# One PSUM bank of a projection taken from another pool: a two-layer hybrid decoder trunk on one NeuronCore

## The chip, the cores and the metric

The kernel runs on one core of a Trainium2 chip. The metric is the device time of one execution in microseconds; the other cores are idle. The engines are named as in the profile: PE (TensorE, matrix multiply; PEld is its weight load), DVE (VectorE), ACT (ScalarE), POOL (GpSimd) and SP (SyncE, which here only issues DMAs). PE accumulates into PSUM, which has eight banks of 128 partitions by 512 float32 in this kernel's use; DVE and ACT read the results out.

## What is computed

512 tokens of width 1024 go through two layers. In each layer one normalised input `h` feeds a gated short convolution (A), a sparse attention with an indexer and a top-k choice of 128 keys (B), a gated linear recurrence in chunks (C) and a cross-attention into 256 memory tokens (M). Each branch is lifted to width 1024, gated, and summed; then come an output projection, a residual, and a SwiGLU feed-forward part with a residual. Cut to what the change touches:

```
h = rmsnorm(x, norm_mix)
(..., d_q, d_k, d_v, ..., g_q, g_f, g_i, g_g, m_q, gate_logits) = split_cols(h @ w_in)
hv  = g_i.reshape(b, s, HG_HEADS, HG_DV)          # the recurrence's values
o_c = hgrn2_chunkwise(hq, hk, hv, log_f)
y_b = dsa_attention(q, k, d_v, iq, ik, iw)        # 8 heads of 64, 4 blocks of 128 queries
merged = sum over n of gates[:, :, n] * (branches[n] @ w_lift[n])
```

## The kernel before, in words

**Products.** All large products are float32 made of three passes of a rounded type: each operand is split into a high and a low part, and `mm3` (L271 to L276) issues high by high, high by low, low by high. A weight matrix comes in chunks (`Chunk`, L214 to L230): SP issues one DMA into `w_raw` (two buffers of 1 MB), then for each piece of 128 by 1024 numbers ACT makes `w_hi` (L226) and DVE makes `w_lo` (L229), three buffers each. Both have a raised priority (AHEAD). In `features` the weight is the stationary operand, so L274 and L275 read `w_hi` and L276 reads `w_lo`. In `tokens_wide` the tokens are stationary and the weight streams.

**Names in the trace.** In a trace row the left name is the tile written and the right ones are read. A row such as `mm<-h_hi,w_hi` does not say which of the two was stationary.

**PSUM.** The eight banks are three pools, each tile one bank: `mm` with three (L103, accumulators of the products), `at` with two (L106, the scores of the attentions) and `tr` with three (L109, transposes and small sums).

```
MM_BUFS = 3
TR_BUFS = 3
AT_BUFS = 2
```

**Values.** `values` (L682 to L691) makes the four token blocks of `hv` from one 1024 by 512 slice of `w_in`. It needs four accumulators at once, one for each block of 128 tokens: the three `mm` banks and one more. `tokens_wide` (L261) walks the four weight pieces and adds each into all four accumulators. ACT then scales every accumulator into `hv` (L688). The first three of these are put into `behind`, and the next `w_hi` pass is ordered after them (L227); the fourth is not.

**Attention.** `attend(t)` (L705 to L738) handles a block of 128 queries in two halves of four heads. For each head, `dots` (L700) issues two small products into an `at` bank (L702, L703), DVE adds the bias, finds the smallest and writes `prob` (L715; five buffers), ACT takes the exponential, DVE inverts the sum (L718), ACT scales. Then PE transposes the four `prob` tiles into `tr` banks (L726), which frees them, and multiplies with the values of the attention into another `tr` bank (L732).

```
for i in range(4):
    ps = at_ps()[:, :n]
    dots(ps, qS, kS, 4 * q + i, t, n)
    p = dp2.tile([P, S], F32, name="prob", bufs=PR_BUFS)[:, :n]
    dve.tensor_tensor_reduce(out=p, in0=ps, in1=biases[t], ...)
```

**What sets the order.** L868 writes the program order of the stage: `values`, then three halves of `attend`, then one step of the lift of branch A (gates, L529, and products, L546), three more halves, and so on. A scheduler takes instructions at compile time by priority (this program order, and AHEAD for the marked ones), engine by engine, as soon as its own model of the timeline holds them ready; it hands out the buffers of a pool in the same walk. The result is one fixed list for each engine, and on the chip each engine works its list strictly in order and waits where a buffer or an input is not there yet. Just ahead of the stage DVE works the last top-k search of the indexer (`select`, L841, L842).

The stage runs once in each layer, at about 307 to 455 us and 1291 to 1440 us of the span.

Of the kernel before, what the change touches and what calls it, by code (L numbers as in the profile page):

```python
# [45 lines left out]
MM_BUFS = 3  # L46
# [23 lines left out]
def hybrid_trunk(ctx: ExitStack, tc: tile.TileContext, x, mem, positions, norm_mix, w_in, conv_w,  # L70
# [19 lines left out]
    def A(dst, src, func, **kw):  # L90
        name = tables.get(func)
        if name is not None and name != table["set"]:
            load = act.preload_act_table_set(name)
            for u in table["users"]:
                tc.add_manual_dep(load.ins, u.name, order, reason="table set")
            table.update(set=name, load=load.ins, users=[])
        i = act.activation(dst, src, func, **kw)  # L97
        if name is not None:
            tc.add_manual_dep(i.ins, table["load"].name, order, reason="table set")
            table["users"].append(i.ins)  # L100
        return i

    def mm_ps():  # L103
        return pmm.tile([P, 512], F32, name="mm")

    def at_ps():  # L106
        return pat.tile([P, 512], F32, name="at", bufs=AT_BUFS)

    def tr_ps():  # L109
        return pat.tile([P, 512], F32, name="tr", bufs=TR_BUFS)  # L110
# [129 lines left out]
    def wchunk(src, kt, n):  # L240
        return Chunk(src, kt, n)
# [19 lines left out]
    def tokens_wide(ws, a, kt, pss):  # L261

        k0 = 0
        for w in ws:
            for ks, _, _ in w.parts:
                for t, ps in enumerate(pss):
                    for k in ks:
                        mm3(ps, pair(a, k0 + k, slice(t * P, (t + 1) * P)), w.at(k), k0 + k == 0, k0 + k == kt - 1)
            k0 += w.kt
# [246 lines left out]
    def mixer(l, h, norms, cm, cf):  # L516
# [164 lines left out]

        def values(hv):  # L682
            ws = [wchunk(w_in[l][k0 * P:(k0 + 4) * P, C_GI:C_GI + 512], 4, 512) for k0 in (0, 4)]
            pss = [mm_ps() for _ in range(MM_BUFS)] + [at_ps()]
            tokens_wide(ws, h, KD, pss)
            for t, ps in enumerate(pss):
                with tc.high_priority(offset=AHEAD):
                    i = A(hv[:, t, :], ps, AF.Copy, scale=r_t[:, t:t + 1])  # L688
                if t < MM_BUFS:
                    behind.append(i)  # L690
            yield  # L691

        with pool_("dsa") as dp:
# [173 lines left out]
            with pool_("att", "left") as dp2:  # L867
                weave(chain(values(hv), lift(0, y_a, merged)), chain(*(attend(t, dp2, y_b) for t in range(NT))), R2)  # L868
# [268 lines left out]
```

## Time and profile before

| what | value |
|---|---|
| median of 3 runs | 2047.54 us (2046.99 to 2047.55) |
| the profiled execution | 2047.71 us |
| span of its instructions | 2045.6 us |
| PE busy | 2031.7 us, 99% of the span |
| DVE busy | 1277.0 us, 62% |
| ACT busy | 1019.9 us, 50% |
| mean DMA rate | 100 GB/s |
| granted TensorE clock, mean | 0.997 |

A row of the timeline gives start, duration, engine, line, operation, tiles, and in brackets the idle time of the engine just before with the instruction that ended it. Matmuls overlap in the pipeline, so their durations overlap too; the distance from one start to the next is what a matmul costs PE. A row of the windows gives the stretch, its length, then busy time (and instructions) of PE, PEld, DVE, ACT and POOL, the granted clock, the share of DMA, and GB/s.

### The profile page before, as it was taken

What the parts mean: (1) busy time and instruction counts of PE and PEld (TensorE: products, weight loads), DVE (VectorE), ACT (ScalarE), POOL (GpSimd) and SP (SyncE); (2) the same over time, 40 slices, a digit from 0 to 9 for tenths busy, and PEclk for the clock granted to TensorE, in tenths of its full rate; (3) what the DMA queues carried; (4) which work ended last, traced back from release to release, by engine and by line L of the source; (5) the groups of instructions that cost most, each with busy time, mean ns of one, the idle gap of its engine ahead of it and who ended that gap; (6) DMA issues with size and microseconds to landing.
All of it is one profiled execution on the core that took longest, in us unless ns stands there. A gap on an engine that the chain in (4) does not pass through costs nothing.

```text
span 2045.6 us, 26194 instructions
## 1 busy us (share of the span) xinstructions
PE 2031.7 (99%) x10156; PEld 1705.9 (83%) x10156; DVE 1277.0 (62%) x2519; ACT 1019.9 (50%) x1836; POOL 9.8 (0%) x33
## 2 busy tenths in 40 slices
PE   8999999999999999999999999999999999999999
PEld 8998987778888888888889898877888788888887
DVE  6779997657686544344457889864777654533442
ACT  7653655866665433223355456486766633322231
POOL 0000000000000000000000000000000000000000
PEclk9999999999999999999999999999999999999999
DMA  7623232212243232233243213222222422323222
GB/s 251 221 85 97 68 103 83 81 54 93 68 128 113 83 103 93 93 104 102 88 155 94 88 57 108 88 62 83 83 83 83 145 87 98 103 73 113 92 83 93
DMA packets 185660, 203.77 MB, mean 100 GB/s; under 512 B 4271, under 2 KB 172289, under 8 KB 185409
## 3 DMA queue, kind: packets, MB, share of 16 engines
q1 hardware_dynamic: 181248, 193.04, 29.7%
q10 hardware_dynamic: 4128, 8.93, 1.2%
q8 instruction: 80, 1.31, 0.3%
q14 instruction: 44, 0.35, 0.1%
q0 software_dynamic: 160, 0.13, 0.0%
HBM read 191.60 MB, written 10.49 MB: 99 GB/s over the span
## 4 chain that ended last, share of the span: by engine, by line
PE 97%; DMA 1%; DVE 1%; ACT 1%; issue 0%; SPq 0%; DVEq 0%
PE mm L274 29%; PE mm L275 29%; PE mm L276 29%; PE tr L732 1%; PE tr L726 1%; PE at L702 1%; PE at L703 1%; PE at L276 1%; PE at L274 1%; PE at L275 1%; DMA w_raw<-in_mem_w_kv_dram 1%; PE at L954 0%; PE at L980 0%; PE tr L668 0%; PE tr L771 0%
## 5 line engine op out<-in xcount | busy, mean ns | idle before, releaser
L229 DVE TENSOR_TENSOR w_lo<-w_raw,w_hi 128x1024 fp32r<-128x1024 f32 (+1 forms) x346 | 419.5, 1213 | 383.2 <-ACT w_hi L97 383.0
L274 PE MATMUL mm<-h_hi,w_hi 128*128 128x512 f32 x1664 | 651.9, 393 | 0.7 <-DVE fg L1081 0.4
L275 PE MATMUL mm<-h_lo,w_hi 128*128 128x512 f32 x1664 | 651.6, 392 | 0.0
L276 PE MATMUL mm<-h_hi,w_lo 128*128 128x512 f32 x1664 | 649.8, 392 | 0.0
L97 ACT ACTIVATE w_hi<-w_raw 128x1024 fp32r<-128x1024 f32 (+1 forms) x346 | 363.2, 1051 | 463.2 <-PE mm L275 397.5
L274 PEld LDWEIGHTS mm<-h_hi,w_hi 128*128 128x128 f32 x1664 | 313.2, 188 | 65.0 <-DVE fg L1081 1.2
L276 PEld LDWEIGHTS mm<-h_hi,w_lo 128*128 128x128 f32 x1664 | 312.9, 188 | 64.6 <-issue 0.6
L275 PEld LDWEIGHTS mm<-h_lo,w_hi 128*128 128x128 f32 x1664 | 313.1, 188 | 63.3 <-issue 1.0
L276 PE MATMUL mm<-w_hi,h_lo 128*128 128x256 f32 (+2 forms) x368 | 109.5, 298 | 0.0
L275 PE MATMUL mm<-w_lo,h_hi 128*128 128x256 f32 (+2 forms) x368 | 109.1, 297 | 0.0
L274 PE MATMUL mm<-w_hi,h_hi 128*128 128x256 f32 (+2 forms) x368 | 108.3, 298 | 0.0
L275 PE MATMUL mm<-a_lo,w_hi 128*128 128x512 f32 x272 | 106.1, 390 | 0.0
L274 PE MATMUL mm<-a_hi,w_hi 128*128 128x512 f32 x272 | 105.9, 389 | 0.0
L276 PE MATMUL mm<-a_hi,w_lo 128*128 128x512 f32 x272 | 105.6, 390 | 0.0
L274 PE MATMUL mm<-y_hi,w_hi 128*128 128x512 f32 x256 | 100.4, 393 | 1.2 <-ACT y_hi L97 1.2
L275 PE MATMUL mm<-y_lo,w_hi 128*128 128x512 f32 x256 | 100.7, 393 | 0.0
L276 PE MATMUL mm<-y_hi,w_lo 128*128 128x512 f32 x256 | 100.3, 392 | 0.0
L97 ACT ACTIVATE a_hi<-fg 128x512 fp32r<-128x512 f32 x44 | 27.8, 633 | 106.9 <-DVE fg L1086 106.9
L97 ACT ACTIVATE prob<-prob,small 128x256 f32<-128x256 f32 (+3 forms) x128 | 69.0, 554 | 14.7 <-DVE small L715 8.6
L275 PEld LDWEIGHTS mm<-w_lo,h_hi 128*128 128x128 f32 x368 | 70.2, 191 | 2.2
L276 PEld LDWEIGHTS mm<-w_hi,h_lo 128*128 128x128 f32 x368 | 70.2, 191 | 1.9
L274 PEld LDWEIGHTS mm<-w_hi,h_hi 128*128 128x128 f32 x368 | 69.9, 191 | 1.9
(377 smaller groups left out, 2982.9 us busy)
## 6 DMA issues: line engine op xcount, KB each, us to landing
w_raw<-in_w_in_dram SPq DMA_DIRECT2D x72, 1024.0 KB, 5.2
w_raw<-in_ffn_w_up_dram SPq DMA_DIRECT2D x44, 1024.0 KB, 5.1
w_raw<-in_w_lift_dram SPq DMA_DIRECT2D x32, 512.0 KB, 3.5
w_raw<-in_ffn_w_down_dram SPq DMA_DIRECT2D x16, 1024.0 KB, 5.3
w_raw<-in_mem_w_kv_dram SPq DMA_DIRECT2D x8, 1024.0 KB, 5.4
w_raw<-in_w_out_dram SPq DMA_DIRECT2D x8, 1024.0 KB, 5.4
w_raw<-in_ffn_w_down_dram SPq DMA_DIRECT2D x10, 512.0 KB, 3.4
kv<-kv ACTq DMA_DIRECT2D x8, 512.0 KB, 3.2
```

What stands on the lines that cost most here:

```text
L97: i = act.activation(dst, src, func, **kw)
L229: dve.tensor_sub(lo, raw[:, k:e], f(hi))
L274: pe.matmul(ps, ah, bh, start=first, stop=False)
L275: pe.matmul(ps, ah, bl, start=False, stop=False)
L276: pe.matmul(ps, al, bh, start=False, stop=last)
L702: pe.matmul(ps, q[:, hh, s], k[0][:, :n], start=True, stop=False)
L703: pe.matmul(ps, q[:, hh, s], k[1][:, :n], start=False, stop=True)
L726: pe.transpose(pp[:, (2 * e + i) * P:(2 * e + i + 1) * P], probs[2 * i + e][:, b * P:(b + 1) * P], ident)
L732: pe.matmul(pv[e * HD:(e + 1) * HD, :], vt[:, b, :], pt[:, b, e * 2 * P:(e + 1) * 2 * P], start=b == 0, stop=b == t)
```

## The change

One line of `values`: its fourth accumulator is a tile of the pool `tr` in place of one of the pool `at`. Nothing else is edited; sizes and numbers of buffers stay, and no instruction is added or taken away. `final` (L1047), which also uses an `at` bank as a fourth accumulator, stays as it is.

```
         def values(hv):
             ws = [wchunk(w_in[l][k0 * P:(k0 + 4) * P, C_GI:C_GI + 512], 4, 512) for k0 in (0, 4)]
-            pss = [mm_ps() for _ in range(MM_BUFS)] + [at_ps()]
+            pss = [mm_ps() for _ in range(MM_BUFS)] + [tr_ps()]
             tokens_wide(ws, h, KD, pss)
```

More of the change, by code (lines that the diff above doesn't have):

```diff
@@ L683, in values @@
             ws = [wchunk(w_in[l][k0 * P:(k0 + 4) * P, C_GI:C_GI + 512], 4, 512) for k0 in (0, 4)]
-            pss = [mm_ps() for _ in range(MM_BUFS)] + [at_ps()]
+            pss = [mm_ps() for _ in range(MM_BUFS)] + [tr_ps()]
             tokens_wide(ws, h, KD, pss)
```

## The prediction, made before the change was run

> **What bounds the kernel now.** I read the page first, then the waits of PE, then the windows and the timeline around the two places where `values` runs.
>
> ```profile
> span 2045.6 us, 26194 instructions
> PE 2031.7 (99%) x10156; PEld 1705.9 (83%) x10156; DVE 1277.0 (62%) x2519; ACT 1019.9 (50%) x1836; POOL 9.8 (0%) x33
> PE 97%; DMA 1%; DVE 1%; ACT 1%; issue 0%; SPq 0%; DVEq 0%
> ...
> PE at L702 <- DVE small L715: 2.4, 6, 0.4
> PE mm L274 <- ACT y_hi L97: 1.2, 1, 1.2
> ```
>
> PE is busy all but 14 us, and the chain that ends last is PE for 97%. So the time is PE's list of matmuls plus its waits, and a wait taken out of PE's list comes off the end unless another takes its place. The longest entry of PE's waits is six waits of the attention's scores (L702) for the DVE reduction L715. The busy shares of the two stages that hold them are in the windows:
>
> ```profile
> 1305.00:1330.00 25.00, 23.83 (x112) 19.52 (x111) 17.05 (x45) 11.97 (x27) 0.00 (x0) 1.00 0.28 85
> 1330.00:1440.00 110.00, 110.00 (x561) 85.87 (x560) 61.84 (x142) 81.73 (x163) 1.49 (x4) 1.00 0.23 72
> ```
>
> Of the 25 us around the end of `values` PE lacks 1.17 us; in the 110 us after it, none. DVE has 61.84 of 110 us to do there and ACT 81.73. The timeline of PE in layer 1 shows where the 1.17 us are:
>
> ```profile
> 1311.57 0.22 PE L702 MATMUL at<-k_hi,qS 128*128 128x128 f32 x1
> ...
> 1317.02 0.39 PE L276 MATMUL at<-w_hi,h_lo 128*128 128x512 f32 x1
> 1317.24 0.22 PE L702 MATMUL at<-k_hi,qS 128*128 128x128 f32 x1
> 1317.30 0.28 PE L703 MATMUL at<-k_lo,qS 128*128 128x128 f32 x1
> 1317.97 0.33 PE L702 MATMUL at<-k_hi,qS 128*128 128x128 f32 x1 [0.39 <-DVE small L715]
> ...
> 1318.80 0.33 PE L702 MATMUL at<-k_hi,qS 128*128 128x128 f32 x1 [0.39 <-DVE small L715]
> ...
> 1319.63 0.33 PE L702 MATMUL at<-k_hi,qS 128*128 128x128 f32 x1 [0.39 <-DVE small L715]
> 1319.79 0.28 PE L703 MATMUL at<-k_lo,qS 128*128 128x128 f32 x1
> 1319.90 0.45 PE L274 MATMUL mm<-h_hi,w_hi 128*128 128x512 f32 x1
> ...
> 1320.87 0.39 PE L276 MATMUL mm<-h_hi,w_lo 128*128 128x512 f32 x1
> ...
> 1322.03 0.39 PE L275 MATMUL mm<-h_lo,w_hi 128*128 128x512 f32 x1
> ...
> 1324.98 0.22 PE L702 MATMUL at<-k_hi,qS 128*128 128x128 f32 x1
> ...
> 1325.38 0.45 PE L275 MATMUL mm<-h_lo,w_hi 128*128 128x512 f32 x1
> ```
>
> The first head's dots run at 1311.57, inside `values`. The last product of `values` starts at 1317.02. Then heads two to five go through one bank, each waiting for the reduction of the one before, and the first gate product (L274) comes at 1319.90. One `at` bank is enough to keep them apart by 0.83 us because the other still holds the fourth accumulator, as ACT's rows show:
>
> ```profile
> 1316.31 0.69 ACT L97 ACTIVATE hv<-mm,rstd_t 128x512 f32<-128x512 f32 x1 [0.44 <-PE mm L276]
> 1316.90 1.99 ACT L97 ACTIVATE w_hi<-w_raw 128x1024 fp32r<-128x1024 f32 x2
> ...
> 1319.17 0.68 ACT L97 ACTIVATE hv<-at,rstd_t 128x512 f32<-128x512 f32 x1
> ```
>
> The fourth accumulator is read out from 1319.17 to 1319.85, so for the whole stall the scores have a single bank.
>
> **The change, part by part.** No instruction is added or removed; a bank moves. Two things follow.
>
> First, the scores have two banks throughout. From 1317.24 to 1319.90 are 2.66 us for four heads. What four heads cost without waits: two of them run from 1324.98 to 1325.38, 0.40 us, so four take 0.80. The stall is thus worth 1.86 us in layer 1, more than the 1.17 us that the records call idle, since their ends are modelled. In layer 0 the same four heads take 333.02 to 335.69, 2.67 us (rows below). Upper bound of the gain: 2 x 1.86 = 3.7 us.
>
> It will not all come back, because the next work, the first gate product, needs weights. DVE's rows:
>
> ```profile
> 1316.33 0.28 DVE L715 CUSTOM_DVE_ANT_0 prob<-at,causal_bias 128x128 f32<-128x128 f32 x1
> ...
> 1317.62 0.29 DVE L715 CUSTOM_DVE_ANT_0 prob<-at,causal_bias 128x128 f32<-128x128 f32 x1 [0.99 <-PE at L703]
> ...
> 1319.49 1.22 DVE L229 TENSOR_TENSOR w_lo<-w_raw,w_hi 128x1024 fp32r<-128x1024 f32 x1
> ...
> 1326.89 0.29 DVE L715 CUSTOM_DVE_ANT_0 prob<-at,causal_bias 128x128 f32<-128x128 f32 x1 [3.38 <-PE tr L726]
> ...
> 1328.61 1.22 DVE L229 TENSOR_TENSOR w_lo<-w_raw,w_hi 128x1024 fp32r<-128x1024 f32 x1 [1.42 <-ACT w_hi L97]
> ```
>
> ACT's first `w_hi` starts at 1316.90 and is one of two in 1.99 us, so it is there at about 1317.9. The pass for `w_lo` takes 1.22 us, and the first product that reads `w_lo` (L276, 1320.87) follows its end (1319.49 + 1.22 = 1320.71) by 0.16. If DVE turns to `w_lo` the moment `w_hi` is there, L276 can start at 1317.9 + 1.22 + 0.16 = 1319.3, 1.6 us earlier than now. I expect two reductions ahead of it instead (head one and two are then reduced from 1316.33 on, under the tail of `values`; three and four follow at 1317.62, about 0.3 us each), so `w_lo` runs from 1318.25 to 1319.47 and L276 starts at 1319.63: 1.24 us earlier. By that point six heads are done instead of five, which saves 0.20 later: 1.44 to 1.8 us a layer. I take 1.6, so **3.2 us** for both layers. Lower bound: if one bank-sized wait is all that goes, a 0.83 us step becomes 0.20, 0.6 us a layer, 1.2 in all; a loss is bounded under the rivals.
>
> Does the earlier start carry to the end? What stands in its way would be weights for the following products. The next `w_lo` pass of this stage that matters starts at 1328.61 and ends at 1329.83; its chunk is first used here:
>
> ```profile
> 1339.45 0.40 PE L274 MATMUL mm<-h_hi,w_hi 128*128 128x512 f32 x1
> ```
>
> That is 9.6 us of cover, against 1.6 us of shift. I cost the knock-on at nothing; without that cover each shifted microsecond would be lost again, at most 3.2.
>
> Second, a `tr` bank is held until about 1319.85 (335.6 in layer 0). Who waits for it? The first row is the readout of the fourth accumulator in layer 0, the second the busy time of all instructions on `tr` tiles from 318 to 335.6 us, the third the first transpose of the stage in layer 1:
>
> ```profile
> 334.95 0.67 ACT L97 ACTIVATE hv<-at,rstd_t 128x512 f32<-128x512 f32 x1
> ...
> 318.00:335.60 17.60, 0.00 (x0) 0.00 (x0) 0.00 (x0) 0.00 (x0) 1.00 0.10 31
> ...
> 1326.58 0.27 PE L726 MATMUL tr<-ident,prob 128*128 128x128 f32 x1
> ```
>
> No one uses `tr` in that time, and the first user comes 6.7 us after the bank is free, with two other banks beside it. Cost: nothing. Were the transposes to come straight after `values`, two banks in place of three would hold a transpose back for one readout, 0.68 us.
>
> Third, the clock, in layer 0 only:
>
> ```profile
> 333.02 0.22 PE L702 MATMUL at<-k_hi,qS 128*128 128x128 f32 x1
> ...
> 335.69 0.49 PE L274 MATMUL mm<-h_hi,w_hi 128*128 128x512 f32 x1
> 335.97 0.63 PE L275 MATMUL mm<-h_lo,w_hi 128*128 128x512 f32 x1
> ...
> 339.38 0.39 PE L275 MATMUL mm<-h_lo,w_hi 128*128 128x512 f32 x1
> ...
> 335.00:337.00 2.00, 1.61 (x7) 1.36 (x7) 1.94 (x6) 2.00 (x6) 0.00 (x0) 0.74 0.00 0
> 337.00:339.00 2.00, 2.00 (x7) 1.54 (x6) 2.00 (x4) 1.40 (x7) 0.00 (x0) 0.50 0.04 5
> ```
>
> Right after the stall the granted clock is 0.50 and the products run 0.43 us apart, from 335.97 to 339.38. From 335.69 to 339.38 are nine steps, 3.69 us; the same nine in layer 1 (1319.90 to 1322.03) take 2.13. So the stall of layer 0 cost another **1.56 us** in clock. Layer 1 had the same stall and kept its clock, so the drop is no certain consequence. With the idle time cut to a third or less I expect it to go. The Trainium skill (TensorE: Matmul & The Clock Gate, Part 1: The HAM clock gate) holds that a free-running window of 3.4 us decides the clock; the slow stretch here, 3.41 us, agrees, and whether a stall falls into one window is then chance. It also asks for an idle window to slow the clock, and here 1.17 us of idle time were enough. By that rule the drop in layer 0 could stay or turn up in layer 1, which is a rival below.
>
> Sum against the profiled execution's own time: 2047.71 - 3.2 - 1.56 = 2042.95. That execution lies 0.17 above the median of the runs (2047.54), so against the median the forecast is **2042.8**.
>
> **The rivals.**
>
> The clock still drops once. Layer 1's undropped stall speaks for chance, the shorter idle time against it. 2042.8 + 1.56 = 2044.4.
>
> The stall only moves. The order of every list is made anew; if the scheduler now places heads five to seven ahead of the gate product, they wait for their banks as before, and DVE reaches `w_lo` later. For it: it placed four heads there before. Against: two banks halve each wait. With the lower bound of 1.2 us and the clock drop kept, 2047.54 - 1.2 = 2046.3.
>
> The change does nothing, because the new lists leave the second bank idle until after the gates. Head one at 1311.57 was put into `values` as soon as a bank was free, which speaks against it. 2047.5.
>
> Slower: reductions ahead of weights in DVE's list. There are five `prob` buffers. The sixth reduction (1326.89) stood idle on DVE for 3.38 us until a transpose freed a buffer; before, no weights that PE needed at once were behind it. With a second bank more heads' dots are done early, their reductions move up in DVE's list, and a `w_lo` pass that PE needs can come to stand behind one. Then PE waits for a reduction (0.29), a pass (1.22) and the handoff (0.16): 1.67 us each time. Sixteen half blocks (eight in each layer) offer the place. Three such waits (5.0) eat the gain; six (10.0) give 2047.5 - 4.8 + 10.0 = 2052.7. For it: every list of a 110 us stage is re-made, and PE has no idle time there now that could be gained. Against: DVE is busy only 61.84 of 110 us, and `w_lo` has priority over reductions.
>
> **How the numbers follow.** Forecast 0.55, clock still drops 0.09, the stall only moves 0.10, nothing 0.06, slower 0.20. About 0.2%, 4.1 us, is what a measurement of this kernel can tell from no change, so faster begins at 2043.4. The forecast's own range is 2041.6 (all 3.7 us, the clock, and half a microsecond unforeseen) to 2043.9 (1.2 us a layer from the weights alone); 0.48 of its 0.55 lie below 2043.4. That gives faster 0.48, slower 0.20 and the rest, 0.32, within. The range leaves out a little below 2041.2 and most of the slower case: 2041.2 to 2050.
>
> **What would show it.** Right: PE's waits no longer list L702 on L715, or at under 0.6 us; two heads' dots stand inside `values`; the first gate product follows the last product of `values` by under 1.7 us (2.88 before); the clock is 1.00 at both places; PE in the 110 us after has no new wait; the fourth accumulator is read as `hv<-tr`. Wrong: PE waits on `w_lo` or `w_hi` in the attention stage, DVE idle on L726 with `w_lo` next in its list, or a clock below 1.00 behind a stall elsewhere.

## The result, and the profile after

| | before | changed |
|---|---|---|
| median of 17 runs each | 2046.51 us (2045.38 to 2047.55) | 2043.15 us (2042.67 to 2043.87) |
| ratio | | 0.9983, 95% interval 0.9976 to 0.9991 |
| span of the profiled execution | 2045.6 us | 2040.9 us |

The kernel is 3.36 us faster. The interval of the ratio does not contain 1; at 0.17% the gain stays just inside the 0.2% that the prediction had set as the mark of "faster". The forecast of 2042.8 missed by 0.35 us, and that it came so near is luck. It took 4.76 us off where 3.36 were measured, 1.40 too much; but it took them off 2047.54, the median of three runs, where the 17 runs have 2046.51, so its start was 1.03 too high. The page, the windows that answer to those of before, and the waits of PE:

```profile
span 2040.9 us, 26188 instructions
PE 2028.1 (99%) x10156; PEld 1704.2 (84%) x10156; DVE 1277.1 (63%) x2519; ACT 1018.5 (50%) x1836; POOL 9.8 (0%) x33
PE 98%; DMA 1%; ACT 1%; DVE 1%; issue 0%; SPq 0%; DVEq 0%
...
PE mm L274 <- ACT y_hi L97: 1.2, 1, 1.2
PE tr L144 <- DVE ones_d L118: 1.1, 1, 1.1
PE tr L396 <- DVE mt_lo L398: 0.8, 2, 0.6
PE at L702 <- DVE small L715: 0.7, 4, 0.2
...
1300.00:1325.00 25.00, 24.66 (x117) 20.32 (x116) 17.62 (x43) 11.00 (x24) 0.00 (x0) 1.00 0.27 85
1325.00:1435.00 110.00, 110.00 (x563) 86.09 (x562) 61.93 (x144) 81.18 (x165) 1.49 (x4) 1.00 0.23 69
```

The six waits of L702 for L715 (2.4 us) are four now (0.7 us). Around the end of `values` PE lacks 0.34 us in place of 1.17, and in the 110 us after it still none. The timeline of PE, ACT and DVE in layer 1:

```profile
1308.05 0.22 PE L702 MATMUL at<-k_hi,qS 128*128 128x128 f32 x1
...
1308.21 0.27 PE L702 MATMUL at<-k_hi,qS 128*128 128x128 f32 x1
...
1313.72 0.39 PE L276 MATMUL tr<-w_hi,h_lo 128*128 128x512 f32 x1
1313.94 0.22 PE L702 MATMUL at<-k_hi,qS 128*128 128x128 f32 x1
...
1314.67 0.33 PE L702 MATMUL at<-k_hi,qS 128*128 128x128 f32 x1 [0.17 <-DVE small L715]
...
1315.50 0.33 PE L702 MATMUL at<-k_hi,qS 128*128 128x128 f32 x1 [0.17 <-DVE small L715]
...
1315.78 0.45 PE L274 MATMUL mm<-h_hi,w_hi 128*128 128x512 f32 x1
...
1316.76 0.40 PE L276 MATMUL mm<-h_hi,w_lo 128*128 128x512 f32 x1
...
1313.60 1.99 ACT L97 ACTIVATE w_hi<-w_raw 128x1024 fp32r<-128x1024 f32 x2
...
1315.88 0.67 ACT L97 ACTIVATE hv<-tr,rstd_t 128x512 f32<-128x512 f32 x1
...
1315.37 2.36 DVE L229 TENSOR_TENSOR w_lo<-w_raw,w_hi 128x1024 fp32r<-128x1024 f32 x2
```

Two heads now run inside `values`, at 1308.05 and 1308.21. Behind it stand five more, two pairs and a single one, with a wait of 0.17 us ahead of the second pair (1314.67) and ahead of the fifth head (1315.50). The first gate product follows the last product of `values` by 2.06 us, where it was 2.88.

To compare kernels I use one figure, the **lost time** of this gap: the distance from the start of the last product of `values` to the start of the first gate product, less 0.23 us for that product itself, less 0.20 us for each head that is done between. Before, it is 2.88 - 0.23 - 4 x 0.20 = 1.85 in layer 1 and 1.87 in layer 0 (2.90 apart); after, 2.06 - 0.23 - 5 x 0.20 = 0.83 in both layers. Unlike the idle time it does not depend on modelled ends, and it charges a kernel nothing for heads that it must do anyway.

### The profile page after: what moved, and what is told of

Its sections match the earlier page's. It is cut to its first block, busy times and chain, and to the rows that moved or that the text cites. A ratio compares the mean times of both kernels' runs of the same rounds, so it can differ in the third digit from the quotient of the medians.

```text
span 2040.9 us, 26188 instructions
## 1 busy us (share of the span) xinstructions
PE 2028.1 (99%) x10156; PEld 1704.2 (84%) x10156; DVE 1277.1 (63%) x2519; ACT 1018.5 (50%) x1836; POOL 9.8 (0%) x33
## 4 chain that ended last, share of the span: by engine, by line
PE 98%; DMA 1%; ACT 1%; DVE 1%; issue 0%; SPq 0%; DVEq 0%
PE mm L274 29%; PE mm L275 29%; PE mm L276 29%; PE tr L732 1%; PE at L702 1%; PE tr L726 1%; PE at L703 1%; PE at L276 1%; PE at L275 1%; PE at L274 1%; DMA w_raw<-in_mem_w_kv_dram 1%; PE at L954 0%; PE at L980 0%; PE tr L668 0%; PE tr L771 0%; PE tr L635 0%
## 5 line engine op out<-in xcount | busy, mean ns | idle before, releaser
L276 PE MATMUL mm<-h_hi,w_lo 128*128 128x512 f32 x1664 | 649.4, 391 | 0.0
L276 PEld LDWEIGHTS mm<-h_hi,w_lo 128*128 128x128 f32 x1664 | 312.6, 188 | 64.1 <-issue 0.2
L276 PE MATMUL mm<-w_hi,h_lo 128*128 128x256 f32 (+2 forms) x368 | 109.5, 298 | 0.0
L276 PE MATMUL mm<-a_hi,w_lo 128*128 128x512 f32 x272 | 105.6, 390 | 0.0
L276 PE MATMUL mm<-y_hi,w_lo 128*128 128x512 f32 x256 | 100.2, 392 | 0.0
L276 PEld LDWEIGHTS mm<-w_hi,h_lo 128*128 128x128 f32 x368 | 70.2, 191 | 1.9
```

Source lines behind the costliest of these rows:

```text
L276: pe.matmul(ps, al, bh, start=False, stop=last)
```

## The experiments

The edits are shown against the kernel before, unless it is said otherwise.

### The kernel before again: is the clock a matter of chance?

No edit.

> The kernel before, unchanged, for the clock of each of its runs (only the profiled one was seen so far). Theory (the clock drop of 1.56 us behind the stall is a matter of chance from run to run): the runs fall into two groups about 1.5 us apart, near 2045.7 and near 2047.3, and the longer ones show a granted clock lower by about 0.001 (3.41 us at half clock in 2045 are 0.0008). Rival (the drop is there in every run, as in the profiled one, and the spread has another cause): one clock in all runs, whatever their length.

Its 11 runs had a median of 2046.93 us: five from 2045.88 to 2046.31, six from 2046.93 to 2047.69. The mean clocks go with this, though not without exception: 0.998 in four of the five short runs and 0.997 in the fifth, the profiled one; 0.997 in five of the six long ones. With the other runs of the kernel before in this study there are 127, in three groups with no run between them: 42 near 2045.85, 70 near 2047.35 and 15 near 2049.28 us. The profiled execution fell into the shortest group. The same stretch of layer 0, in the execution before the prediction (first row) and in this one (second row), with the clock third from the end:

```profile
330.00:345.00 15.00, 13.82 (x59) 11.15 (x58) 7.70 (x24) 9.86 (x23) 0.00 (x0) 0.89 0.33 105
```

```profile
330.00:345.00 15.00, 13.82 (x68) 11.24 (x67) 7.81 (x24) 10.04 (x23) 0.00 (x0) 1.00 0.34 106
```

The stall is the same in both, 13.82 us of PE in 15, but only the first paid in clock; from the first gate product to the first product of the recurrence (L954) the two need 131.58 and 129.99 us. So the drop comes by chance, as the theory had it. That the three groups are runs with no drop, with one and with two is argued from their distances (1.50 and 1.93 us) and from the next two kernels. It is not shown: no run of the longest group was traced, and no trace has a drop behind the stall of layer 1.

Where chance comes in, the slow stretches tell. In the execution before the prediction they begin at 8.28, 15.11 and 335.96 us and last 3.41 us each; their distances are 2 and 96 times 3.413 us, so they keep to one raster from the start of the program on. The stall of layer 0, 333.02 to 335.69, lay whole in the period that ended at 335.96. In the execution of this run the raster lies otherwise: a slow stretch begins at 9.59, and 95 periods later, at 333.85, a boundary cuts the stall (333.35 to 336.01) in two. The Trainium skill (TensorE: Matmul & The Clock Gate, Part 1: The HAM clock gate) says that the window is free-running, and the trace agrees with it in that.

With the groups read as no drop, one and two there are on average (70 + 2 x 15) / 127 = 0.79 drops in a run. Whatever they are, the mean of all 127 runs is 2047.09, 1.24 us above the middle of the shortest group.

### One layer at a time

```
-            pss = [mm_ps() for _ in range(MM_BUFS)] + [at_ps()]
+            pss = [mm_ps() for _ in range(MM_BUFS)] + [tr_ps() if l == 0 else at_ps()]
```

> The changed bank in layer 0 only. Theory (each layer gains by its own stall, 1.23 us, and layer 0 its share of a clock drop that comes in about half the runs, 0.8 us): 1.2 to 2.1 us below before, about 2044.7, and PE's list after the stage of layer 0 gains nothing further. Rival (the gain is that of the re-made lists of the attention stage, not of the stall): no fixed share; the gain then appears between the end of the stall and the end of the stage. Rival (all of the gain is clock, lost in layer 0): the full 3.4 us.

Median 2045.07 us, ratio 0.9992 (0.9983 to 1.0001); the interval contains 1. Eight runs lie from 2044.55 to 2045.16 and three near 2046.7. Lost time 0.83 in layer 0 and 1.86 in layer 1.

```
-            pss = [mm_ps() for _ in range(MM_BUFS)] + [at_ps()]
+            pss = [mm_ps() for _ in range(MM_BUFS)] + [at_ps() if l == 0 else tr_ps()]
```

> The changed bank in layer 1 only. Theory: 1.2 us from the stall of layer 1, plus whatever clock drops that layer had (none in the profiled run): 1.2 to 2.0 below before, about 2045.0; with the layer 0 kernel the two gains add to about 3.4. Rival (all of the gain is clock in layer 0): no difference from before.

Median 2044.77 us, ratio 0.9990 (0.9981 to 0.9999); again three of the eleven runs stand apart, from 2046.30 to 2046.69, where the other eight end at 2045.19. Lost time 1.87 and 0.83. The profiled execution, 2046.53 us, is one of the three, and its window in layer 0, where this kernel keeps the stall, has the drop:

```profile
330.00:345.00 15.00, 13.82 (x59) 11.12 (x58) 7.61 (x24) 9.96 (x23) 0.00 (x0) 0.89 0.34 105
```

The medians lie 2.2 and 2.5 us below that of the kernel before on the same chip (2047.28), more than the theory's 2.1 and 2.0, because the median of the kernel before is a run of the middle group and theirs are not. From shortest group to shortest group (2045.85 before; the eight lower runs here have medians of 2044.99 and 2044.59) the gains are 0.9 and 1.3, near the 1.03 that the lost time gives one layer. So the gain is no clock effect of layer 0 alone. That each layer that keeps the stall keeps its chance of a drop is what the two sets of three runs speak for.

One side effect: in the first of the two the list of layer 1 was also made anew, though nothing there was edited. From the first gate product of layer 1 to the norm at its end it needs 366.9 us against 366.4 of the kernel before. Half a microsecond of this kind turns up again below.

### The suspected cost doubled, which came out as a gain

```
-            pss = [mm_ps() for _ in range(MM_BUFS)] + [at_ps()]
+            pss = [mm_ps() for _ in range(2)] + [at_ps() for _ in range(2)]
...
-                if t < MM_BUFS:
+                if t < 3:
```

> The suspected cost doubled: values takes two accumulators from mm and both banks of at, so the scores have none until a readout. Theory (the price is the number of score banks that values holds while PE has nothing else): the head that ran inside values now runs behind it too, one more step of 0.83 in place of 0.20 us, 0.6 us a layer, and the clock drops more often: 0.6 to 2.5 us above before. Rival (only the list order matters): the stall between the last product of values and the first gate product stays at 2.9 us.

Median 2044.25 us, ratio 0.9986 (0.9978 to 0.9995): 3.0 us below the kernel before on the same chip, and 1.6 below its shortest group, not above. As I had put it, the theory falls, and so does the rival, since the stall does not stay at 2.9 us. PE in layer 0:

```profile
332.46 0.39 PE L276 MATMUL at<-w_hi,h_lo 128*128 128x512 f32 x1
332.69 0.22 PE L702 MATMUL at<-k_hi,qS 128*128 128x128 f32 x1
...
333.42 0.33 PE L702 MATMUL at<-k_hi,qS 128*128 128x128 f32 x1 [0.39 <-DVE small L715]
...
333.69 0.45 PE L274 MATMUL mm<-h_hi,w_hi 128*128 128x512 f32 x1
```

With no bank to be had, the list holds only two heads between `values` and the gates, with a single wait, and the gates come after 1.23 us. Lost: 1.23 - 0.23 - 2 x 0.20 = 0.60. So the price is not how many banks are held. In the kernels so far it is **how many heads the list puts into the gap, times what each waits there**. That the missing bank is what kept the heads out of the gap is how I read the list; no run tests it alone.

### The bank left in `at`, but read out sooner

```
-                if t < MM_BUFS:
+                if t < NT:
```

> The kernel before with the bank left in at, but its readout ordered ahead of the next weights like the other three. Theory (what costs is a score's step through one bank while PE has nothing else; lost time = distance from the last product of values to the first gate product, less 0.23, less 0.20 for each head between: 1.86 before, 0.83 after): the bank is free about 1.3 us sooner, the weights come 0.6 us later, six heads stand between; lost about 1.1 a layer, 1.5 to 2.3 us below before with its share of the clock. Rival (the bank must not be in at at all): the 1.86 and the 0.39 us waits stay.

Median 2047.25 us, ratio 1.0005 (0.9996 to 1.0014): nothing gained. Seven runs lie from 2046.93 to 2047.30 and four from 2049.01 to 2049.34; the four, 2.2 us apart from the others, were not traced. The seven have a median of 2046.99, 1.1 above the shortest group of the kernel before. The figure explains it: lost 2.29 in both layers in place of the 1.1 expected, six heads over 3.72 us. The rival has the waits of 0.39 us right, but the lost time did not stay at 1.86, it grew. Layer 0, ACT first and then PE:

```profile
332.78 0.69 ACT L97 ACTIVATE hv<-at,rstd_t 128x512 f32<-128x512 f32 x1
...
333.30 0.33 PE L702 MATMUL at<-k_hi,qS 128*128 128x128 f32 x1 [0.39 <-DVE small L715]
334.13 0.33 PE L702 MATMUL at<-k_hi,qS 128*128 128x128 f32 x1 [0.39 <-DVE small L715]
334.96 0.33 PE L702 MATMUL at<-k_hi,qS 128*128 128x128 f32 x1 [0.39 <-DVE small L715]
335.24 0.27 PE L702 MATMUL at<-k_hi,qS 128*128 128x128 f32 x1
```

The bank is read out by 333.47, yet the heads at 334.13 and 334.96 still wait for one another. Only the head at 335.24 does without a wait. The rows fit what was said of the scheduler: which bank a head uses is settled when the lists are made, so a bank that comes free early on the chip helps no head that was given the other one. My expectation had let the heads take whatever is free.

### Two accumulators in `tr`

```
-            pss = [mm_ps() for _ in range(MM_BUFS)] + [at_ps()]
+            pss = [mm_ps() for _ in range(2)] + [tr_ps() for _ in range(2)]
...
-                if t < MM_BUFS:
+                if t < 2:
```

> Two accumulators of values in mm, two in tr; the scores have both banks. The lists are those of the changed kernel but for the two heads that stood inside values and now stand behind it, seven in the gap. Theory: one more pair step of 0.83 for 0.40 us of work, so lost 1.26 in place of 0.83 a layer, 0.9 us above the changed kernel, about 2.5 below before; one tr bank left is enough for 10 us. Rival (a held tr bank costs): transposes wait, and the loss shows after the gap.

Median 2043.72 us, ratio 0.9985 (0.9976 to 0.9994). The distance is 2.89 us with seven heads in it, lost 2.89 - 0.23 - 1.40 = 1.26, as expected to the hundredth, and the time lies 0.5 above the changed kernel's (expected 0.9), though the two did not run side by side. From the first gate product to the norm at the end of the mixer both kernels need the same within 0.05 us. In layer 0 the two lent banks are held from 308.2 to 334.6 us, and the first transpose comes at 344.0, so the bank that is left for so long costs nothing.

### Three accumulators in `tr`, with and without the order of the readouts

Without it:

```
-            pss = [mm_ps() for _ in range(MM_BUFS)] + [at_ps()]
+            pss = [tr_ps() for _ in range(TR_BUFS)] + [mm_ps()]
...
-                if t < MM_BUFS:
-                    behind.append(i)
```

> Three accumulators in tr, one in mm, and no order of readouts before weights: the gates' banks and weights do not depend on the readouts. Two heads stand between values and the gates. Theory (what is left of the stall, 0.83 a layer, is heads put into a gap that the gates' weights leave): the gap shrinks to about 0.6, lost about 0.1 to 0.4, 1 to 1.5 us below the changed kernel. Rival (the weights are bound by their buffers, not by the readouts): the gate products wait for weights, no gain.

Median 2042.51 us, ratio 0.9978 (0.9969 to 0.9987), the best of the study. PE and ACT in layer 0 (the dots stand on L700 here, two lines having gone):

```profile
332.33 0.39 PE L276 MATMUL mm<-w_hi,h_lo 128*128 128x512 f32 x1
332.56 0.22 PE L700 MATMUL at<-k_hi,qS 128*128 128x128 f32 x1
...
332.73 0.27 PE L700 MATMUL at<-k_hi,qS 128*128 128x128 f32 x1
...
332.95 0.45 PE L274 MATMUL mm<-h_hi,w_hi 128*128 128x512 f32 x1
...
327.38 1.06 ACT L97 ACTIVATE w_hi<-w_raw 128x1024 fp32r<-128x1024 f32 x1 [4.44 <-PE mm L276]
332.76 1.06 ACT L97 ACTIVATE w_hi<-w_raw 128x1024 fp32r<-128x1024 f32 x1 [4.32 <-PE mm L276]
333.73 1.82 ACT L97 ACTIVATE hv<-tr,rstd_t 128x512 f32<-128x512 f32 x3
```

The gap is gone: 0.62 us for two heads, lost 0.62 - 0.23 - 0.40 = 0. ACT makes the first `w_hi` of the gates at 327.38, five us before `values` ends, where in the changed kernel it starts at 332.56, behind three readouts. The accumulators are read out from 333.73 on, which holds up nobody, since the gates have two free `mm` banks. The time is 0.7 below the changed kernel's 2043.22, where 1 to 1.5 was expected.

The changed kernel without that order, its banks as they are:

```
-                if t < MM_BUFS:
-                    behind.append(i)
```

> The changed kernel without the order of the three readouts ahead of the next weights; the gate products stand directly behind values, no head between. Theory: lost under 0.3 a layer, 1 us below the changed kernel. Rival (that order is there because ACT would otherwise hold the gates' accumulators): PE waits for a readout at the first gate product, 0.7 to 1.5 us a layer, and the time is that of the changed kernel or above.

Median 2046.22 us, ratio 0.9996 (0.9987 to 1.0005). The rival is right:

```profile
332.67 0.39 PE L276 MATMUL tr<-w_hi,h_lo 128*128 128x512 f32 x1
334.78 0.50 PE L274 MATMUL mm<-h_hi,w_hi 128*128 128x512 f32 x1 [1.72 <-ACT hv L97]
...
333.10 1.06 ACT L97 ACTIVATE w_hi<-w_raw 128x1024 fp32r<-128x1024 f32 x1 [4.78 <-PE tr L276]
334.06 1.83 ACT L97 ACTIVATE hv<-mm,rstd_t 128x512 f32<-128x512 f32 x3
```

Weights and heads are out of the way, but the gates need an `mm` bank, and ACT reads the first one out only at 334.06, behind a weight pass that itself waited for `values` to end. PE stands still for 1.72 us.

The other half of that pair, three `tr` banks with the order put back:

```
-            pss = [mm_ps() for _ in range(MM_BUFS)] + [at_ps()]
+            pss = [tr_ps() for _ in range(TR_BUFS)] + [mm_ps()]
```

> The same banks with the order of readouts ahead of weights put back. Theory (what empties the gap is that the gates' weights are made before values ends, which needs the order gone; the free mm banks alone let nothing start): seven heads stand in the gap again, distance 2.9, lost 1.26 a layer, 2043.7. Rival (the free mm banks are what counts): the distance stays at 0.6 and the time at 2042.5.

Median 2043.91 us, ratio 0.9986 (0.9977 to 0.9995); distance 2.89, seven heads, lost 1.26: the theory to the hundredth. Free `mm` banks alone bring nothing (lost 1.26, in the changed kernel 0.83), weights made early alone do harm (1.88); together they empty the gap. On the same chip the changed kernel and the best one ran again:

> The changed kernel again, on one chip with the three below. Theory: 2043.2, none of its runs 1.5 us longer than the rest (no clock drop, since PE's idle time behind values is 0.34 us a layer).

Median 2043.34 us (2042.56 to 2044.34), ratio 0.9984 (0.9975 to 0.9993), as expected: the highest run is 1.0 above the median.

> The kernel with three accumulators in tr, one in mm and no order of readouts, again beside the changed kernel. Theory: its gap holds no wait, 0.5 to 0.8 us below the changed kernel, as the first look had it across chips. Rival: the difference was one of chips, below 0.2.

Median 2042.61 us (2042.41 to 2043.11), ratio 0.9979 (0.9970 to 0.9987). It beats the changed kernel by 0.7 us, as expected, but by less than the 1.66 us by which its lost time is smaller. From the first gate product to the norm it needs 364.69 and 367.47 us in the two layers, the changed kernel beside it 363.02 and 365.82. In each layer 1.00 us of that difference is the five heads that it has still to do there; the other 0.67 and 0.65 eat most of the gain.

### The fourth readout ahead of the weights, bank in `tr`

```
-                if t < MM_BUFS:
+                if t < NT:
```

(in the changed kernel)

> The changed kernel with the fourth readout, now of the tr bank, also ordered ahead of the weights. Theory (the weights are what the gap waits for, the bank is not): the fourth readout delays the weights by 0.6 us, lost 1.0 to 1.3 in place of 0.83, 0.3 to 1 us above the changed kernel. Rival (a tr bank held long costs): below the changed kernel.

Median 2044.94 us, ratio 0.9991 (0.9982 to 1.0000), 1.6 above the changed kernel on the same chip. The direction is the theory's; the size (0.3 to 1 expected) and the place are not. Lost is 0.89 in layer 0 and 0.88 in layer 1, hardly more than 0.83, where 1.0 to 1.3 was expected. From the first gate product to the norm it needs 363.97 us in layer 0 and 366.53 in layer 1, where the changed kernel needs 363.03 and 365.82. That is 1.6 us in stages in which the waits of PE grow by only 0.1 us.

### All of them side by side

| kernel | distance, us | heads between | lost, a layer | median, us | median less both layers' lost | gates to norm, both layers, us |
|---|---|---|---|---|---|---|
| before (shortest group) | 2.89 | 4 | 1.86 | 2045.85 | 2042.1 | 732.4 |
| changed (28 runs) | 2.06 | 5 | 0.83 | 2043.22 | 2041.6 | 731.7 |
| two in `mm`, two in `at` | 1.23 | 2 | 0.60 | 2044.25 | 2043.1 | 733.3 |
| fourth readout first, `at` (its seven lower runs) | 3.72 | 6 | 2.29 | 2046.99 | 2042.4 | 732.9 |
| two in `mm`, two in `tr` | 2.89 | 7 | 1.26 | 2043.72 | 2041.2 | 731.6 |
| three in `tr`, order | 2.89 | 7 | 1.26 | 2043.91 | 2041.4 | 731.7 |
| fourth readout first, `tr` | 2.11 | 5 | 0.88 | 2044.94 | 2043.2 | 733.3 |
| three in `tr`, no order | 0.62 | 2 | 0.00 | 2042.51 | 2042.5 | 733.0 |
| changed, no order | 2.11 | 0 | 1.88 | 2046.22 | 2042.5 | 732.7 |

The column before the last would be one number if the gap were all. It spreads over 2.0 us, from 2041.2 to 2043.2. The last column shows where that lies: it is the time from the first gate product to the norm at the end of the mixer, plus 0.20 us for each head already done before the gates, from the traces. It spreads over 1.7 us and orders the kernels in nearly the same way. So it is the part that the re-made lists of the attention and recurrence stages put in or take out; the waits of PE in that time differ by at most 0.35 us between the kernels. Which property of a list costs the rest is open.

## Why the prediction was right, point by point

**What bounds the kernel.** Right. The waits of the scores were the ones to go, and what went came off the end.

**The second score bank.** The mechanism was right: two heads inside `values`, the rest in pairs, no new wait. The term of 3.2 us was too large. The lost time fell from 1.86 to 0.83, 1.03 a layer and **2.06 us** for both. Two sizes in it were wrong. The step that failed is "so `w_lo` runs from 1318.25 to 1319.47 and L276 starts at 1319.63: 1.24 us earlier". It has two reductions ahead of `w_lo` and four heads in the gap. In the changed kernel three reductions (1314.32, 1314.54, 1315.15) and five heads stand there, so L276 starts 3.04 us after the last product of `values` (1316.76 less 1313.72), where the forecast had 2.61 and the kernel before 3.85: it is 0.81 us earlier. And the 0.20 us credited for a sixth head is no gain, since the second head inside `values` makes `values` longer by as much: from the first of these heads to the last product of `values` there are 5.67 us, 5.45 before.

Nor is it `w_hi` that sets when the gates start. It is there 1.0 us after 1313.60, at about 1314.6, but the first gate product starts at 1315.78, directly behind the fifth head. In the two kernels with seven heads the distance grew to 2.89, and in the one with two accumulators in `tr` `w_hi` is there 2.2 us before the gates. Whether the list keeps the gates behind the heads, or behind the `w_lo` pass that stands behind the reductions of these heads in DVE's list, the runs do not separate: in all three kernels the first `w_lo` pass starts 0.41 or 0.42 us before the first gate product.

**The clock.** Counted as 1.56 us on the strength of one execution. The size of a drop was right (131.58 less 129.99 is 1.59), and so was that it hangs on the stall: the 28 runs of the changed kernel form no group 1.5 us above the others. But it is no loss that every run pays; averaged over 127 runs it is worth **1.24 us**.

**The knock-on, counted as nothing.** Nearly right: the cover held, PE waits for no weights. The mean of all runs fell from 2047.09 to 2043.24, by 3.85 us; 2.06 of that is the gap and 1.24 the clock, which leaves **0.55 us** that the re-made lists gave on top. The traces have 0.73 us for it between the first gate product and the norm, 0.59 in layer 0 and 0.14 in layer 1 (the last column above). The sign is luck: other lists of the same stages gave up to 1.1 us back.

**The held `tr` bank.** Right at nothing. Two and even three of these banks can be lent: from the first gate product to the norm these kernels (the one with three, with the order kept) need what the changed kernel needs, within 0.05 us in each layer.

**The rivals.** "The clock still drops once" did not come: no such group among 28 runs. "The stall only moves" is what the lists did in part, five heads ahead of the gates, though each pair shares one wait. "Nothing" is excluded. "Slower" did not come. Of the reductions it feared, one moved up in DVE's list: the fifth, which came behind the first `w_lo` pass of the gates (first row, kernel before) and now stands ahead of it, at 1315.15. The sixth did not; it comes at 1325.91, behind four `w_lo` passes of which the last starts at 1324.17, where it had come ahead of the fourth.

```profile
1320.63 0.28 DVE L715 CUSTOM_DVE_ANT_0 prob<-at,causal_bias 128x128 f32<-128x128 f32 x1
...
1315.15 0.29 DVE L715 CUSTOM_DVE_ANT_0 prob<-at,causal_bias 128x128 f32<-128x128 f32 x1 [0.31 <-PE at L703]
...
1324.17 1.23 DVE L229 TENSOR_TENSOR w_lo<-w_raw,w_hi 128x1024 fp32r<-128x1024 f32 x1 [4.92 <-ACT w_hi L97]
...
1325.91 0.28 DVE L715 CUSTOM_DVE_ANT_0 prob<-at,causal_bias 128x128 f32<-128x128 f32 x1
```

**The final figure.** 4.76 us were forecast and 3.36 measured in the first comparison, 3.85 over all runs. From the middle group (2047.35), whose runs are like the one that the forecast started from, to the changed kernel's 2043.22 it is 4.13: 1.50 of clock, 2.06 of the gap and 0.57 of the lists. So of the 1.14 us that the gap fell short, half was made up by a gain that was not forecast. Of the six signs named as "right", the gap came out at 2.06 where I had set 1.7, and the waits at 0.7 us in place of 0.6; the clock, the heads inside `values`, the 110 us without a wait and the readout `hv<-tr` held.

## What to carry to other kernels

Where a scheduler writes fixed lists, ask of a borrowed buffer not how long it is held but what the list places into the gap that it causes: a kernel with fewer score banks beat the one before, with fewer heads in the gap. A readout that must precede a weight pass and a weight pass that must precede a product form one chain; it opens only if both the accumulators and the order are changed. And a single profile can hold a chance event: run the kernel before several times and look for groups before a term is taken from one trace.

## What was not expected of the hardware

The clock fell in about four passes of ten (0.79 drops over two stalls, with the groups read as above) through a stall in which PE idled for 1.17 us, in three pieces over the 2.67 us from 333.02 to 335.69. In the kernel with one unbroken idle time of 1.72 us (2.11 from product to product) the eleven runs spread over 1.1 us and form no group 1.5 us apart. So the length of the idle time alone does not decide.

Where the stall lies on the raster of 3.413 us has a part in it. Of the six traced stalls of the kernel before's kind, two lay whole in one period, those of layer 0 in the execution before the prediction and in the kernel changed in layer 1 only (333.12 to 335.79, slow from 336.33), and behind both the clock fell. Four were cut by a boundary, at 1319.00 in the first of these executions, at 333.85 and 1316.89 in the kernel before again and at 1314.39 in the kernel changed in layer 0 only, and behind none it fell. But this is not the whole rule. A stall of 2.67 us lies whole in a period in (3.41 - 2.67) / 3.41 = 0.22 of the passes, an estimate from these rows, fewer than four in ten; and the idle 1.72 us lay whole in one period in both layers, and the clock stayed at 1.00. What else decides, the runs here do not show.
